# Feature-major products with act hi and lo as one 512-column operand in four banks

## The chip, the cores and the metric

The kernel runs on one core of a Trainium2 chip. The time is device microseconds of that core for one execution of the whole program; lower is better. Of the engines, PE does the matrix products (PEld are its weight loads), DVE and ACT the elementwise work, SP starts the transfers from device memory.

## The reference, cut to what matters

Two layers over 256 tokens of width 2048, all in float32. Layer A is a stick-breaking attention with 16 heads of 128, layer B a latent attention whose keys and values come from a compressed latent of 512.

```python
def mixer_a(h, w_in, w_out):
    q, k, v, g = jnp.split(h @ w_in, 4, axis=-1)
    o = stick_breaking_attention(heads(q), heads(k), heads(v)).reshape(b, s, SB_WIDTH)
    return (o * jax.nn.silu(g)) @ w_out
...
def mixer_b(h, kv, w_in, q_latent_norm, w_uq, w_out, cos, sin):
    cq, g = jnp.split(h @ w_in, [Q_LORA_RANK], axis=-1)
    q = (rms_norm(cq, q_latent_norm) @ w_uq).reshape(b, s, MLA_HEADS, QK_HEAD_DIM)
...
    o = mla_attention(q_nope, q_rope, k_nope, k_rope, v).reshape(b, s, MLA_WIDTH)
    return (o * jax.nn.silu(g)) @ w_out
...
for each layer:
    out = mixer(rms_norm(x, norm_pre))
    x = x + rms_norm(out, norm_post)
    x = x + (p @ w_ple_proj) * jax.nn.sigmoid(x @ w_ple_gate)
```

## The kernel before, in words

**Numbers in two parts.** PE multiplies in a reduced float32 (fp32r). Each operand is therefore held as hi, the rounded value, and lo, what is missing: `split` makes hi by an ACT copy and lo by a DVE subtraction (lines 81 to 87). A product is hi·hi + hi·lo + lo·hi: `mm3` (line 108) issues these three matmuls, lines 109 to 111, onto the same part of a PSUM bank.

**Units.** Weights come in units of 128 x 1024 floats (512 KB). `unit` (line 89) starts the transfer on SP into one of four `raw` buffers, then ACT makes `whi` and DVE `wlo`, four buffers each. Eight units make one group: 2048 rows of weights by 512 columns, which are four blocks of 128 columns (four heads). One unit holds two of the 16 row slices k.

**Two kinds of product.** `rows` (line 113) gives token-major results: activations are loaded as weights, 512 weight columns move, one bank per 128 tokens. `cols` (line 123) gives feature-major results: a 128 x 128 weight block is loaded and the 256 tokens move, so that two blocks share one bank of 512 floats. It runs over k outside and the four blocks inside, and all blocks of a group end with the last unit. `cols` makes the gates of both layers (`gate_group`, and the three loops from line 239), k and q of layer A (`group_a`, line 330) and the products with `w_uk` and `w_uq` (`group_b`, line 545, one unit for two blocks at four k). `rows` makes v, the outputs, the latents and the other gates.

**PSUM.** There are eight banks, four named `acc` and four `att`. A `cols` group takes two `acc` banks, so two groups fit; the third gate group of layer A takes two `att` banks (line 256). Behind a group, DVE multiplies each bank by a row of rms factors, 512 columns at a time (lines 221 and 337), or copies it (line 550); a gate then gets its silu on ACT (line 223).

**Activations.** `act_t` (line 161) holds the transposed activations, all of hi and then all of lo: [128, 2, 16, 256]. `latT` (line 488) does the same for the two latents.

**Order.** The program text gives each instruction its priority; the order on each engine's queue is set at build time by a scheduler that, whenever an engine comes free in its simulated time, takes the earliest instruction that is ready there. On the chip every queue is then served in that order. `weave` (line 136) lays three steps of each of the last group's four heads between the units of the next group: for layer A after units 1, 7, 13 and 19 and two and four units later.

Of the kernel before, what the change touches and what calls it, by code (L numbers as in the profile page):

```python
# [9 lines left out]
F32 = mybir.dt.float32  # L10
F32R = mybir.dt.float32r
BF16 = mybir.dt.bfloat16
AF = mybir.ActivationFunctionType
ALU = mybir.AluOpType
AX = mybir.AxisListType

P = 128
# [29 lines left out]
def hybrid_trunk(ctx: ExitStack, tc: tile.TileContext, a: dict):  # L47
# [11 lines left out]
    def acc():  # L59
        return psum.tile([P, SLAB], F32, tag="acc", name="acc", bufs=4)  # L60
# [59 lines left out]
            ts = slice(t * P, (t + 1) * P)  # L120
            mm3(accs[t], aT[0][:, k, ts], aT[1][:, k, ts], hi[:, c], lo[:, c], k == 0, k == ktot - 1)

    def cols(banks, aT, w, k0, nk, nblk, ktot):

        hi, lo = w
        for kk in range(nk):
            k = k0 + kk
            for i in range(nblk):
                c = slice((kk * nblk + i) * P, (kk * nblk + i + 1) * P)
                mm3(banks[i // 2][:, i % 2 * T:(i % 2 + 1) * T], hi[:, c], lo[:, c], aT[0][:, k, :], aT[1][:, k, :],  # L130
                    k == 0 and i % 2 == 0, k == ktot - 1 and i % 2 == 1, skip_group_check=True)

    def pair(ap):
        return ap.rearrange("p (k t) -> p k t", k=2)
# [24 lines left out]


    def act_t():
        b = big.tile([P, 2, NK, T], F32R, tag="actT", name="actT", bufs=2)
        return b[:, 0], b[:, 1]

    def transpose_pair(j):

# [42 lines left out]

    silus = []  # L210

    def gate_group(g, aT, sg, get, row):
        o = [acc(), acc()]
        for u in range(8):
            cols(o, aT, get(u), 2 * u, 2, GRP, NK)
        gate_out(g, o, sg, row)

    def gate_out(g, o, sg, row):
        for i in range(2):
            gt = tmp.tile([P, 2, T], F32, tag="t512", name="gt", bufs=2)  # L220
            nc.vector.tensor_tensor(gt, pair(o[i]), row, ALU.mult)
            h = g * GRP + 2 * i
            silus.append(nc.scalar.activation(sg[:, h:h + 2, :], gt, AF.Silu))

    def warm_up(n):

# [7 lines left out]
    hT = act_t()  # L234
    xs = big.tile([P, NK, T], F32, tag="tok", name="xs", bufs=3)
    sgA = big.tile([P, NH, T], F32, tag="sg", name="sgA", bufs=1)
    o0, o1 = [acc(), acc()], [acc(), acc()]
    warm_up(WARM)
    for u in range(8):
        nc.sync.dma_start(out=xs[:, 2 * u:2 * u + 2, :], in_=pair(a["xT"][u]))  # L240
        w = unit_ga(0, u, parts=2 if u == 0 else 1)
        for k in (2 * u, 2 * u + 1):
            split_gain(hT[0][:, k, :], hT[1][:, k, :], xs[:, k, :], pre[:, 0, k:k + 1])
        cols(o0, hT, w, 2 * u, 2, GRP, NK)

    ssq0 = ssq_tile("ssq0")
    c1 = const.tile([P, P + NK + 2 * NR + NT * 2 * ROPE], F32, name="c1")
    c2 = tmp.tile([P, 2 * P + CHUNK], F32, tag="e", name="c2", bufs=2)
    for u in range(8):
        cols(o1, hT, unit_ga(1, u), 2 * u, 2, GRP, NK)  # L250
        if u in (1, 4, 7):
            load_x(u // 3)
        if u == 6:
            after(nc.sync.dma_start(out=c1, in_=a["c1"]), loads[-1], "the weights go first")
    ident = c1[:, :P]
    o2 = [att(), att()]
    for u in range(8):
        cols(o2, hT, unit_ga(2, u), 2 * u, 2, GRP, NK)
        if u == 0:
            after(nc.sync.dma_start(out=c2, in_=a["c2"]), loads[-1], "the weights go first")  # L260
        if u == 2:
            load_x(3)
        if u == 4:
            rstd0 = rstd_of(ssq0, D, "rstd0")
            rrow0 = rstd_row(rstd0)
            gate_out(0, o0, sgA, rrow0)
            gate_out(1, o1, sgA, rrow0)
    gate_out(2, o2, sgA, rrow0)
    rrow0q = tmp.tile([P, 2, T], F32, tag="rrow", name="rrow0q", bufs=2)
    nc.vector.tensor_scalar(rrow0q, rrow0, SCALE_A, None, ALU.mult)  # L270

# [7 lines left out]
    trir = const.tile([P, P], F32R, name="trir")  # L279
    nc.vector.tensor_copy(trir, c2[:, :P])  # L280

    gate_group(3, hT, sgA, lambda u: unit_ga(3, u), rrow0)


    W3 = T + P
# [3 lines left out]
    after(exp_ln, silus[-1], "the table set of the attention comes after the gates'")  # L289

    def finish_head(h, o, sg, yT):
        y = tmp.tile([P, T], F32, tag="t256", name="y", bufs=2)
        nc.vector.tensor_tensor(y, o, sg[:, h, :], ALU.mult)
        split(yT[0][:, h, :], yT[1][:, h, :], y)

# [33 lines left out]

    def group_a(g, q, k, v):  # L330
        for dst, base, row in ((k, NG, rrow0), (q, 0, rrow0q)):
            o = [acc(), acc()]
            for u in range(8):
                cols(o, hT, unit(a["w_in_a"][(base + g) * 8 + u]), 2 * u, 2, GRP, NK)
                yield
            for i in range(2):
                nc.vector.tensor_tensor(dst[:, 2 * i:2 * i + 2, :], pair(o[i]), row, ALU.mult)
        o = [acc(), acc()]
        for u in range(8):
            rows(o, hT, unit(a["w_in_a"][(2 * NG + g) * 8 + u]), 2 * u, 2, SLAB, NK)  # L340
            yield
        for t in range(NT):
            nc.scalar.activation(v[:, t, :], o[t], AF.Copy, scale=rstd0[:, t:t + 1])
# [118 lines left out]
    def rotate(dst, src, t, n):  # L462

        hw = ROPE // 2
        cs = rope[:, t, 0:1, :].to_broadcast([P, n, ROPE])
        nc.vector.tensor_tensor(dst, src, cs, ALU.mult)
        u = tmp.tile([P, GRP, ROPE], F32, tag="t256", name="rot", bufs=2)[:, :n, :]
        for lo_, hi_ in ((0, hw), (hw, 0)):
            sn = rope[:, t, 1:2, lo_:lo_ + hw].to_broadcast([P, n, hw])
            nc.vector.tensor_tensor(u[:, :, lo_:lo_ + hw], src[:, :, hi_:hi_ + hw], sn, ALU.mult)  # L470
        nc.vector.tensor_tensor(dst, dst, u, ALU.add)

    krt = tmp.tile([P, NT, 2, ROPE], F32, tag="t256", name="krt", bufs=2)
    for t in range(NT):
        rotate(krt[:, t, 0:1, :], ckv[:, t:t + 1, RANK:], t, 1)
        nc.vector.tensor_copy(krt[:, t, 1, :], krt[:, t, 0, :])
# [6 lines left out]

    sgB = big.tile([P, NH, T], F32, tag="sg", name="sgB", bufs=1)
    for g in range(NG):
        gate_group(g, x2T, sgB, lambda u: unit_b(1 + g, u), rrow2)

    latT = big.tile([P, 2, 2, NR, T], F32R, tag="tok", name="latT", bufs=3)
    for i, src in ((0, ckv), (1, cq)):
        sl = ssq_tile(f"sl{i}", 1)  # L490
        for t in range(NT):
            sumsq(sl[:, t, :], src[:, t, :RANK])
        rl = rstd_of(sl, RANK, f"rl{i}")
        for t in range(NT):
            nc.vector.tensor_scalar(src[:, t, :RANK], src[:, t, :RANK], rl[:, t:t + 1], None, ALU.mult)
        for j in range(NR // 2):
            b = att()
            for kk in range(2):
                k = 2 * j + kk
                for t in range(NT):  # L500
                    nc.tensor.transpose(b[:, kk * T + t * P:kk * T + (t + 1) * P], src[:, t, k * P:(k + 1) * P], ident)
            for kk in range(2):
                k = 2 * j + kk
                split_gain(latT[:, i, 0, k, :], latT[:, i, 1, k, :], b[:, kk * T:(kk + 1) * T], qln[:, i, k:k + 1])
    ckvT, cqT = [(latT[:, i, 0], latT[:, i, 1]) for i in range(2)]


    yT = act_t()
# [36 lines left out]
    def group_b(g, q, qr, k, v):  # L545
        for dst, src, aT in ((k, a["w_uk"], ckvT), (q, a["w_uq"], cqT)):
            for i in range(GRP // 2):
                o = acc()
                cols([o], aT, unit(src[g * (GRP // 2) + i]), 0, NR, 2, NR)
                nc.vector.tensor_copy(dst[:, 2 * i:2 * i + 2, :], pair(o))  # L550
                yield
        w = unit(a["w_uqr"][g])
        o = [acc()[:, :T], acc()[:, :T]]
# [123 lines left out]
```

## Time and profile before

| | |
|---|---|
| median of 3 runs | 1056.81 us (1056.16 to 1056.97) |
| the profiled execution | 1058.96 us, its span 1057.2 us |
| granted clock of PE, mean | 0.998 |
| busy: PE, DVE, ACT | 1048.3, 608.9, 540.2 us |
| matmuls, and as many weight loads | 6715 |
| HBM | 178 GB/s over the span |

The profiled execution is 2.15 us longer than the median; 1.76 us of it lie outside the span. Matmuls overlap in the records, so PE's busy time says only that PE had something to do; what one costs is read from the distance between starts.

### The profile page before, as it was taken

To read this page: it belongs to the slowest core of one execution; us is meant where nothing else is said; L and a number is where in the kernel's file an instruction comes from. 1 tells how busy PE (TensorE), PEld (TensorE's weight loads), DVE (VectorE), ACT (ScalarE), POOL (GpSimd) and SP (SyncE) were. 2 spreads that over 40 slices of the span, in tenths; PEclk is the share of its full clock that TensorE was granted. 3 is DMA by queue.
4 is the path that set the end of the run, shared out by engine and by line. 5 is a ranking of instruction groups with operands and counts; after the bars stand their busy time and mean duration, and the time that the engine had idled before them with its cause. 6 is when DMAs were issued, how large, how long until landed. Compare 5 with 4: busy or idle time off the path is not lost.

```text
span 1057.2 us, 16656 instructions
## 1 busy us (share of the span) xinstructions
PE 1048.3 (99%) x6715; PEld 954.1 (90%) x6715; DVE 608.9 (58%) x832; ACT 540.2 (51%) x792; POOL 6.8 (1%) x10
## 2 busy tenths in 40 slices
PE   8999999999999999999999999999999999999998
PEld 7999999989989988888888899999999988788888
DVE  6455444554554545555766576555777765558554
ACT  6545334455445446545555565544555554446442
POOL 0000000000000000000000000000000000000000
PEclk9999999999999999999999999999999999999999
DMA  8855555555555554575665476656544344655662
GB/s 315 278 180 179 182 185 189 162 161 175 164 163 175 171 171 158 166 211 170 201 189 175 134 239 189 188 182 180 161 139 140 115 146 153 196 184 190 213 209 79
DMA packets 55821, 189.17 MB, mean 179 GB/s; under 512 B 6208, under 2 KB 6976, under 8 KB 55744
## 3 DMA queue, kind: packets, MB, share of 16 engines
q1 hardware_dynamic: 55600, 188.09, 56.8%
q8 instruction: 52, 0.85, 0.3%
q14 instruction: 25, 0.20, 0.1%
q10 hardware_dynamic: 144, 0.02, 0.0%
HBM read 185.99 MB, written 2.10 MB: 178 GB/s over the span
## 4 chain that ended last, share of the span: by engine, by line
PE 98%; DMA 1%; DVE 0%; ACT 0%; SPq 0%; issue 0%
PE acc L109 29%; PE acc L110 29%; PE acc L111 29%; PE att L300 1%; PE att L110 1%; PE att L111 1%; PE att L109 1%; PE att L171 1%; PE att L301 1%; PE att L518 1%; PE att L308 1%; DMA raw<-in_w_in_a_dram 1%; PE att L523 1%; PE att L539 0%; PE att L517 0%; PE att L324 0%
## 5 line engine op out<-in xcount | busy, mean ns | idle before, releaser
L83 DVE TENSOR_TENSOR wlo<-raw,whi 128x1024 fp32r<-128x1024 f32 (+1 forms) x295 | 358.5, 1217 | 306.0 <-ACT whi L82 305.3
L82 ACT ACTIVATE whi<-raw 128x1024 fp32r<-128x1024 f32 (+1 forms) x295 | 310.7, 1053 | 342.0 <-PE acc L111 177.8
L109 PE MATMUL acc<-whi,actT 128*128 128x512 f32 (+2 forms) x736 | 277.4, 378 | 0.8 <-DVE osb L390 0.8
L111 PE MATMUL acc<-whi,actT 128*128 128x512 f32 (+2 forms) x736 | 277.3, 378 | 0.0
L110 PE MATMUL acc<-wlo,actT 128*128 128x512 f32 (+2 forms) x736 | 277.1, 377 | 0.0
L109 PE MATMUL acc<-actT,whi 128*128 128x256 f32 x960 | 273.4, 285 | 1.5 <-ACT whi L82 1.5
L110 PE MATMUL acc<-actT,whi 128*128 128x256 f32 x960 | 272.5, 284 | 0.0
L111 PE MATMUL acc<-actT,wlo 128*128 128x256 f32 x960 | 271.5, 284 | 0.5 <-DVE wlo L83 0.5
L109 PEld LDWEIGHTS acc<-actT,whi 128*128 128x128 f32 x960 | 184.7, 192 | 2.5 <-ACT whi L82 2.4
L111 PEld LDWEIGHTS acc<-actT,wlo 128*128 128x128 f32 x960 | 184.3, 193 | 0.9 <-DVE wlo L83 0.9
L110 PEld LDWEIGHTS acc<-actT,whi 128*128 128x128 f32 x960 | 184.8, 192 | 0.1
L109 PEld LDWEIGHTS acc<-whi,actT 128*128 128x128 f32 x736 | 138.4, 188 | 25.1 <-DVE osb L390 1.2
L110 PEld LDWEIGHTS acc<-wlo,actT 128*128 128x128 f32 x736 | 138.5, 188 | 24.1
L111 PEld LDWEIGHTS acc<-whi,actT 128*128 128x128 f32 x736 | 138.2, 188 | 24.1
L87 DVE SCALAR_TENSOR_TENSOR wlo<-raw,pre,whi 128x512 fp32r<-128x512 f32 x80 | 56.8, 748 | 41.6 <-ACT whi L86 41.6
L86 ACT ACTIVATE whi<-raw,pre 128x512 fp32r<-128x512 f32 x80 | 53.5, 715 | 49.7 <-PE acc L110 28.6
L110 PE MATMUL acc<-latT,whi 128*128 128x256 f32 x128 | 36.4, 286 | 0.3 <-DVE latT L87 0.3
L111 PE MATMUL acc<-latT,wlo 128*128 128x256 f32 x128 | 36.4, 286 | 0.0
L109 PE MATMUL acc<-latT,whi 128*128 128x256 f32 x128 | 36.2, 287 | 0.2 <-ACT latT L86 0.2
L110 PEld LDWEIGHTS acc<-latT,whi 128*128 128x128 f32 x128 | 24.4, 191 | 0.5 <-DVE latT L87 0.5
L109 PEld LDWEIGHTS acc<-latT,whi 128*128 128x128 f32 x128 | 24.2, 191 | 0.4 <-ACT latT L86 0.4
L111 PEld LDWEIGHTS acc<-latT,wlo 128*128 128x128 f32 x128 | 24.4, 191 | 0.0
(236 smaller groups left out, 958.6 us busy)
## 6 DMA issues: line engine op xcount, KB each, us to landing
raw<-in_w_in_a_dram SPq DMA_DIRECT2D x127, 512.0 KB, 3.6
raw<-in_w_in_b_dram SPq DMA_DIRECT2D x40, 512.0 KB, 3.9
raw<-in_w_out_a_dram SPq DMA_DIRECT2D x32, 512.0 KB, 3.7
raw<-in_w_pg_a_dram SPq DMA_DIRECT2D x32, 512.0 KB, 3.6
raw<-in_w_out_b_dram SPq DMA_DIRECT2D x32, 512.0 KB, 3.6
raw<-in_w_pg_b_dram SPq DMA_DIRECT2D x24, 512.0 KB, 3.6
raw<-in_w_dkv_dram SPq DMA_DIRECT2D x16, 288.0 KB, 2.9
raw<-in_w_pp_dram SPq DMA_DIRECT2D x8, 512.0 KB, 3.6
```

The costliest lines, as they stand in the source:

```text
L82: nc.scalar.activation(hi, src, AF.Copy)
L83: nc.vector.tensor_tensor(lo, src, hi.bitcast(F32), ALU.subtract)
L86: nc.scalar.activation(hi, src, AF.Copy, scale=gain)
L87: nc.vector.scalar_tensor_tensor(lo, src, gain, hi.bitcast(F32), ALU.mult, ALU.subtract)
L109: nc.tensor.matmul(out, lhsT=sh, rhs=mh, start=start, stop=False, **kw)
L110: nc.tensor.matmul(out, lhsT=sh, rhs=ml, start=False, stop=False, **kw)
L111: nc.tensor.matmul(out, lhsT=sl, rhs=mh, start=False, stop=stop, **kw)
L171: nc.tensor.transpose(b[:, kk * T + t * P:kk * T + (t + 1) * P], x[:, t, k * P:(k + 1) * P], ident)
L300: nc.tensor.matmul(o, lhsT=v[:, 0, c], rhs=w[:, :T], start=True, stop=False)
L301: nc.tensor.matmul(o[:, P:], lhsT=v[:, 1, c], rhs=w[:, T:], start=False, stop=True)
L308: mm(z[:, :T], lhsT=k[:, hh, :P], rhs=q[:, hh, :], start=True, stop=False, skip_group_check=True)
L518: mm(s[:, P:], lhsT=q[:, hh, P:], rhs=k[:, hh, :], start=False, stop=False, skip_group_check=True)
```

## The change

The activations are stored by k, with hi and lo beside each other: [128, 16, 2, 256]. `cols` multiplies the hi part of a weight block with both at once, 512 columns into a whole bank, the left half hi·hi and the right half hi·lo; the lo part of the block is multiplied with act hi, 256 columns, onto the left half. One block now fills one bank, a group four. The new `halves` copies the right half out of the bank on ACT and adds the left half to it on DVE, into the destination; the row factor is then applied in place in SBUF. `cols` now runs over blocks outside and k inside. `cols_stream` gives it one unit at a time, but units 0 and 1 together, and 6 and 7 together: there a block's products over four k stand in a row before the next block's. Gate group 0 of layer A, which loads its activations with its weights, goes unit by unit. `halves` uses a third `t256` buffer, and gate group 2 of layer A uses `acc` banks.

```diff
-    def cols(banks, aT, w, k0, nk, nblk, ktot):
-        hi, lo = w
-        for kk in range(nk):
-            k = k0 + kk
-            for i in range(nblk):
-                c = slice((kk * nblk + i) * P, (kk * nblk + i + 1) * P)
-                mm3(banks[i // 2][:, i % 2 * T:(i % 2 + 1) * T], hi[:, c], lo[:, c], aT[0][:, k, :], aT[1][:, k, :],
-                    k == 0 and i % 2 == 0, k == ktot - 1 and i % 2 == 1, skip_group_check=True)
+    def cols(banks, aT, ws, k0, nk, ktot):
+        n = len(banks)
+        for i, o in enumerate(banks):
+            for m in range(len(ws) * nk):
+                hi, lo = ws[m // nk]
+                k = k0 + m
+                c = slice((m % nk * n + i) * P, (m % nk * n + i + 1) * P)
+                nc.tensor.matmul(o, lhsT=hi[:, c], rhs=aT[2][:, k].rearrange("p i t -> p (i t)"), start=k == 0,
+                                 stop=False, skip_group_check=True)
+                nc.tensor.matmul(o[:, :T], lhsT=lo[:, c], rhs=aT[0][:, k, :], start=False, stop=k == ktot - 1,
+                                 skip_group_check=True)
+    def cols_stream(banks, aT, get):
+        for us in ((0, 1), (2,), (3,), (4,), (5,), (6, 7)):
+            cols(banks, aT, [get(u) for u in us], 2 * us[0], 2, NK)
+            for _ in us:
+                yield
+    def halves(dst, banks):
+        for i, o in enumerate(banks):
+            b = tmp.tile([P, T], F32, tag="t256", name="half", bufs=3)
+            nc.scalar.copy(b, o[:, T:])
+            nc.vector.tensor_tensor(dst[:, i, :], o[:, :T], b, ALU.add)
...
     def act_t():
-        b = big.tile([P, 2, NK, T], F32R, tag="actT", name="actT", bufs=2)
-        return b[:, 0], b[:, 1]
+        b = big.tile([P, NK, 2, T], F32R, tag="actT", name="actT", bufs=2)
+        return b[:, :, 0, :], b[:, :, 1, :], b
...
     silus = []
-    def gate_group(g, aT, sg, get, row):
-        o = [acc(), acc()]
-        for u in range(8):
-            cols(o, aT, get(u), 2 * u, 2, GRP, NK)
-        gate_out(g, o, sg, row)
-    def gate_out(g, o, sg, row):
+    def banks4():
+        return [acc() for _ in range(GRP)]
+    def gate_group(g, aT, sg, get):
+        o = banks4()
+        for _ in cols_stream(o, aT, get):
+            pass
+        halves(sg[:, GRP * g:GRP * (g + 1), :], o)
+    def gate_out(g, sg, row):
...
-            gt = tmp.tile([P, 2, T], F32, tag="t512", name="gt", bufs=2)
-            nc.vector.tensor_tensor(gt, pair(o[i]), row, ALU.mult)
-            h = g * GRP + 2 * i
-            silus.append(nc.scalar.activation(sg[:, h:h + 2, :], gt, AF.Silu))
+            h = sg[:, GRP * g + 2 * i:GRP * g + 2 * i + 2, :]
+            nc.vector.tensor_tensor(h, h, row, ALU.mult)
+            silus.append(nc.scalar.activation(h, h, AF.Silu))
...
-    o0, o1 = [acc(), acc()], [acc(), acc()]
+    o = banks4()
...
     for u in range(8):
...
-        cols(o0, hT, w, 2 * u, 2, GRP, NK)
+        cols(o, hT, [w], 2 * u, 2, NK)
+    halves(sgA[:, :GRP, :], o)
...
-    for u in range(8):
-        cols(o1, hT, unit_ga(1, u), 2 * u, 2, GRP, NK)
+    o = banks4()
+    for u, _ in enumerate(cols_stream(o, hT, lambda u: unit_ga(1, u))):
         if u in (1, 4, 7):
...
         if u == 6:
...
-    o2 = [att(), att()]
-    for u in range(8):
-        cols(o2, hT, unit_ga(2, u), 2 * u, 2, GRP, NK)
+    halves(sgA[:, GRP:2 * GRP, :], o)
+    o = banks4()
+    for u, _ in enumerate(cols_stream(o, hT, lambda u: unit_ga(2, u))):
         if u == 0:
...
         if u == 2:
...
         if u == 4:
...
-            gate_out(0, o0, sgA, rrow0)
-            gate_out(1, o1, sgA, rrow0)
-    gate_out(2, o2, sgA, rrow0)
+            gate_out(0, sgA, rrow0)
+            gate_out(1, sgA, rrow0)
+    halves(sgA[:, 2 * GRP:3 * GRP, :], o)
+    gate_out(2, sgA, rrow0)
...
-    gate_group(3, hT, sgA, lambda u: unit_ga(3, u), rrow0)
+    gate_group(3, hT, sgA, lambda u: unit_ga(3, u))
+    gate_out(3, sgA, rrow0)
...
-        y = tmp.tile([P, T], F32, tag="t256", name="y", bufs=2)
+        y = tmp.tile([P, T], F32, tag="t256", name="y", bufs=3)
...
     def group_a(g, q, k, v):
...
-            o = [acc(), acc()]
-            for u in range(8):
-                cols(o, hT, unit(a["w_in_a"][(base + g) * 8 + u]), 2 * u, 2, GRP, NK)
-                yield
+            o = banks4()
+            yield from cols_stream(o, hT, lambda u: unit(a["w_in_a"][(base + g) * 8 + u]))
+            halves(dst, o)
...
-                nc.vector.tensor_tensor(dst[:, 2 * i:2 * i + 2, :], pair(o[i]), row, ALU.mult)
+                d = dst[:, 2 * i:2 * i + 2, :]
+                nc.vector.tensor_tensor(d, d, row, ALU.mult)
...
         for u in range(8):
...
-        u = tmp.tile([P, GRP, ROPE], F32, tag="t256", name="rot", bufs=2)[:, :n, :]
+        u = tmp.tile([P, GRP, ROPE], F32, tag="t256", name="rot", bufs=3)[:, :n, :]
...
-    krt = tmp.tile([P, NT, 2, ROPE], F32, tag="t256", name="krt", bufs=2)
+    krt = tmp.tile([P, NT, 2, ROPE], F32, tag="t256", name="krt", bufs=3)
...
-        gate_group(g, x2T, sgB, lambda u: unit_b(1 + g, u), rrow2)
-    latT = big.tile([P, 2, 2, NR, T], F32R, tag="tok", name="latT", bufs=3)
+        gate_group(g, x2T, sgB, lambda u: unit_b(1 + g, u))
+        gate_out(g, sgB, rrow2)
+    latT = big.tile([P, 2, NR, 2, T], F32R, tag="tok", name="latT", bufs=3)
...
-                split_gain(latT[:, i, 0, k, :], latT[:, i, 1, k, :], b[:, kk * T:(kk + 1) * T], qln[:, i, k:k + 1])
-    ckvT, cqT = [(latT[:, i, 0], latT[:, i, 1]) for i in range(2)]
+                split_gain(latT[:, i, k, 0, :], latT[:, i, k, 1, :], b[:, kk * T:(kk + 1) * T], qln[:, i, k:k + 1])
+    ckvT, cqT = [(latT[:, i, :, 0, :], latT[:, i, :, 1, :], latT[:, i]) for i in range(2)]
...
     def group_b(g, q, qr, k, v):
...
-                o = acc()
-                cols([o], aT, unit(src[g * (GRP // 2) + i]), 0, NR, 2, NR)
-                nc.vector.tensor_copy(dst[:, 2 * i:2 * i + 2, :], pair(o))
+                o = [acc(), acc()]
+                cols(o, aT, [unit(src[g * (GRP // 2) + i])], 0, NR, NR)
+                halves(dst[:, 2 * i:2 * i + 2, :], o)
```

## Rows read from the trace of the kernel before

**Rows 1.** The page, busy us of each engine, share of the span, instructions.

```profile
PE 1048.3 (99%) x6715; PEld 954.1 (90%) x6715; DVE 608.9 (58%) x832; ACT 540.2 (51%) x792; POOL 6.8 (1%) x10
```

**Rows 2.** The page, chain that ended last, share of the span by line.

```profile
PE acc L109 29%; PE acc L110 29%; PE acc L111 29%; PE att L300 1%; PE att L110 1%; PE att L111 1%; PE att L109 1%; PE att L171 1%; PE att L301 1%; PE att L518 1%; PE att L308 1%; DMA raw<-in_w_in_a_dram 1%; PE att L523 1%; PE att L539 0%; PE att L517 0%; PE att L324 0%
```

**Rows 3.** Waits of PE: who waited for whom, us in total, times, longest.

```profile
PE acc L109 <- ACT whi L82: 1.5, 2, 1.3
PE att L229 <- DVE zeros L149: 1.2, 1, 1.2
PE acc L109 <- DVE osb L390: 0.8, 1, 0.8
PE acc L111 <- DVE wlo L83: 0.5, 1, 0.5
```

**Rows 4.** Windows: length, busy us (instructions) of PE, PEld, DVE, ACT, POOL; clock, DMA.

```profile
25.00:120.00 95.00, 95.00 (x794) 95.00 (x794) 47.43 (x50) 44.95 (x58) 0.69 (x1) 1.00 0.65 210
120.00:400.00 280.00, 280.00 (x1950) 262.97 (x1949) 142.76 (x154) 133.66 (x171) 0.00 (x0) 1.00 0.56 173
740.00:860.00 120.00, 119.56 (x860) 111.03 (x859) 86.45 (x188) 68.26 (x137) 0.00 (x0) 1.00 0.47 142
```

**Rows 5.** Groups by line and form: count, busy us, mean ns; idle before.

```profile
L109 PE MATMUL acc<-actT,whi 128*128 128x256 f32 x960 | 273.4, 285 | 1.5 <-ACT whi L82 1.5
...
L109 PE MATMUL acc<-latT,whi 128*128 128x256 f32 x128 | 36.2, 287 | 0.2 <-ACT latT L86 0.2
L109 PE MATMUL att<-actT,whi 128*128 128x256 f32 x64 | 18.2, 284 | 0.0
```

**Rows 6.** Window, PE alone: us, busy, matmuls, granted clock, DMA share, GB/s.

```profile
655.00:735.00 80.00, 80.00 (x669) 1.00 0.60 185
```

**Rows 7.** Timeline of PE where kinds meet: start, recorded length, instruction.

```profile
148.33 0.28 PE L111 MATMUL acc<-actT,wlo 128*128 128x256 f32 x1
148.45 0.40 PE L109 MATMUL acc<-whi,actT 128*128 128x512 f32 x1
148.68 0.40 PE L110 MATMUL acc<-wlo,actT 128*128 128x512 f32 x1
148.92 0.39 PE L111 MATMUL acc<-whi,actT 128*128 128x512 f32 x1
...
170.01 0.39 PE L111 MATMUL acc<-whi,actT 128*128 128x512 f32 x1
170.24 0.28 PE L109 MATMUL acc<-actT,whi 128*128 128x256 f32 x1
170.35 0.28 PE L110 MATMUL acc<-actT,whi 128*128 128x256 f32 x1
```

**Rows 8.** Groups by line and form, DVE and ACT.

```profile
L83 DVE TENSOR_TENSOR wlo<-raw,whi 128x1024 fp32r<-128x1024 f32 x291 | 355.7, 1224 | 303.4 <-ACT whi L82 302.8
L82 ACT ACTIVATE whi<-raw 128x1024 fp32r<-128x1024 f32 x291 | 308.1, 1059 | 338.2 <-PE acc L111 174.5 <-PE acc L110 135.3 <-issue 12.0
...
L550 DVE COPY arena<-acc 128x512 f32<-128x512 f32 x16 | 11.0, 688 | 8.3 <-PE acc L111 8.1
...
L531 ACT ACTIVATE pr<-att,st 128x256 f32<-128x256 f32 x16 | 7.5, 471 | 0.0
...
L293 DVE TENSOR_TENSOR y<-att,sgA 128x256 f32<-128x256 f32 x16 | 6.8, 424 | 15.3 <-PE att L301 15.3
```

**Rows 9.** Timeline of ACT in group 1: first and last of one attention step.

```profile
193.51 0.47 ACT L313 ACTIVATE e<-att 128x384 f32<-128x384 f32 x1
...
195.72 0.53 ACT L82 ACTIVATE sph<-sp 128x384 fp32r<-128x384 f32 x1 [0.62 <-DVE sp L317]
```

**Rows 10.** Timeline of PE at the first product with `w_uk`.

```profile
742.66 0.39 PE L110 MATMUL acc<-latT,whi 128*128 128x256 f32 x1 [0.28 <-DVE latT L87]
```

**Rows 11.** Timeline of DVE where k of group 0 ends.

```profile
124.89 1.41 DVE L337 TENSOR_TENSOR qkvA<-acc,rrow 128x512 f32<-128x512 f32 x2
126.58 1.23 DVE L83 TENSOR_TENSOR wlo<-raw,whi 128x1024 fp32r<-128x1024 f32 x1 [0.28 <-ACT whi L82]
```

## The prediction

> **What bounds the kernel now.** I read the busy times of the page first [rows 1]: PE is busy 99% of the span, DVE 58%, ACT 51%. The chain that ended last says the same more strictly [rows 2]: 87% of the span lies on lines 109 to 111, the three products of `mm3`, and the rest of that row is nearly all PE too. PE hardly ever waits: the four largest kinds of its waits come to 4.0 us, most of it at the start [rows 3]. In three stretches that the change touches (gates of A, heads of A, first part of the heads of B), PE is busy all the time or all but half a microsecond, while DVE stands at 50 to 72% [rows 4]. So the time is the sum of what PE's instructions take, and only a change in that sum, or a new wait of PE, can move the end.
>
> The mean duration of a matmul (285 ns for 256 columns [rows 5]) is not its price, since the records overlap. The price is the distance from start to start. From 655 to 735 us PE does nothing but feature-major products, 669 in 80.00 us [rows 6]: 119.6 ns each, and I use 120 ns. The token-major products with 512 moving columns start 0.23 us apart [rows 7]; a 256 with 0.11 to 0.12 beside them. I use 227 ns: 120 and the 107 ns that 256 more columns take at the granted clock (1.00, the 2.4 GHz level [rows 6]). So each of these instructions costs about 13 ns beside its columns, however many it has, with a weight load for each in both cases.
>
> **The change, part by part.**
>
> *Products.* Before, one weight block at one k takes three instructions of 256 columns: 3 x 120 = 360 ns. After, it takes one of 512 and one of 256: 227 + 120 = 347 ns. The columns stay the same; one instruction and its weight load are gone. Saved: 13 ns. How many: 960 into acc from actT, 128 from latT and 64 into att [rows 5], 1152 in all (gates 512, q and k of layer A 512, uk and uq 128). 1152 x 13 ns = **15.0 us**. The mixed order stands in the trace only where a group of one kind follows the other: a 256 and then a 512 at 148.33, a 512 and then a 256 at 170.01 [rows 7]. They start 0.12 and 0.23 us apart, so neither neighbour costs the other anything. The ends: with the dearest spacing of these rows (0.24 for a 512 and 0.12 for a 256) 360 ns and nothing is saved; with the cheapest (0.23 and 0.11) 340 ns and 23 us. I take 347 because the 669 products and the same differences on both sides of a transition stand behind it.
>
> *Copies and adds (`halves`).* Each block now needs a 256-column ACT copy out of its bank and a 256-column DVE add: 96 of each. Nearest rows: 471 ns for an ACT pass over 256 out of a bank, 424 ns for a DVE product of that size [rows 8]; I take 0.47 and 0.42 us. ACT gains 96 x 0.47 = 45 us, so 585 us of some 1042, 56%. DVE gains 96 x 0.42 = 40 us less the 16 copies of 0.69 us [rows 8] that go, so some 638 us, 61%. The products with the rms row stay, from SBUF instead of a bank. The tightest stretch, 740 to 860 us, holds 32 of the adds and loses the 16 copies: 86.5 + 13.4 - 11.0 = 89 us of 117, 76%. No queue becomes the bound; the work is hidden under PE, and without that cover the 85 us would count.
>
> *Banks.* A gate, k or q group held two of four accumulator banks, and the next group took the other two. Now it holds all four, and the next group's block i waits for bank i. There are 16 such turnovers: four behind the gates of A, four from k to q, four from q to v, four behind the gates of B. What hides them is the block order at both ends: a pair of units is 16 x 0.347 = 5.55 us, the banks fall due 1.39 us apart, and each is wanted 4.16 us after its last product. Copy and add take 0.89 us; behind one weight split on each queue (1.06 and 1.22 us [rows 8]) they take 3.17 us, which fits. Where an attention step stands ahead on ACT (Abs to the split of sp, 193.51 to 196.25 us, 2.74 us [rows 9]), it is 5.9 us, 1.7 too late. That can meet the three turnovers from k to q in groups 1 to 3, where the first step of a head is due in unit 7. Lower end 0, upper end 5 us; I take 0.5, since ACT has gaps between these steps. After group 0 of the gates, whose last unit is not paired, the banks fall due 0.69 us apart and the first has 2.1 us: it fits with one split half done.
>
> *Units.* A pair wants its second unit 2.2 us earlier and gives both weight buffers back at its end. Four buffers: at a turnover two are held by units 6 and 7 and two by the next 0 and 1, which were split in the buffers of 4 and 5, long free. Units 2 and 3 are split only when the pair ends; they are ready about 2.3 and 3.5 us later, and unit 2 is wanted 5.55 us later. With the last add and two row products on DVE ahead (0.42 + 1.38) it is 4.1 us. I cost it at nothing; it is late by 0.65 us if everything, an attention step's 2 us of DVE too, stands before both splits.
>
> *Order.* The pairs move head steps one unit later, and c2's load on SP behind one more weight load; x's third and c1's loads likewise at most one unit. Nobody needs them within 2.8 us, so nothing. The third `t256` buffer costs no time. At the start PE waits for arriving weights (1.5 and 0.5 us [rows 3]); the first unit is taken block by block, which may cost or give up to 0.8 us; I take 0.
>
> *Into uk.* At 742.66 a product already waited 0.28 us for the latent's split [rows 10]. The two last gate units now release their weight buffers together, so one more split on each queue (up to 2.3 us) can stand ahead of the latent's. Ends 0 and 2.3; I take 0.5, the wait that this row shows, near twice over.
>
> **Sum**, against the profiled execution's own 1058.96 us: -15.0 + 0.5 + 0.5 = 1044.96. The runs' median, 1056.81, is 2.15 us below the profiled one, so **1042.8 us**, 1.3% faster. A measurement of this kernel tells some 0.2% (2.1 us) from no change.
>
> **Rivals.**
>
> 1. *The turnover takes the place of the saving: slower.* If the four copies stand on ACT behind a weight split that is itself released only by the pair's end, the stagger is lost: block 0 of the next group waits for a split, a copy and an add, 1.06 + 0.47 + 0.42 = 1.95 us. Times 16 that is 31 us: 1042.8 - 0.5 + 31 = 1073. It decides from 15/16 = 0.94 us per turnover on. For it: ACT's queue is served in order, and no group has a spare bank. Against it: the evacuation of k at 124.89 started before the next split on DVE at 126.58 [rows 11], and the copies come first in the program. Chance 0.06. The Trainium skill (Perfetto Trace Analysis, Optimizing Tensor Performance) speaks for this rival: independent groups should rotate through different banks so that one's evacuation overlaps the next one's products. By that rule the change gives up an overlap that the kernel before has.
>
> 2. *Units or banks come late, but little: still faster.* At each turnover both splits are 0.65 us late: 10 us, so 1042.8 + 10 = 1053. For it: DVE's share rises everywhere. Against it: slack of 1.4 us or more without attention work. Chance 0.09.
>
> 3. *The change does not save what it says.* If a 512 that alternates with a 256 costs 240 ns, the pair costs the old 360 ns, and with 1 us of new waits the time is 1058. Against it: the two transitions [rows 7], where a 512 before a 256 takes 0.23. Chance 0.05. The Trainium skill (TensorE: Matmul & The Clock Gate, Back-to-back issue gap) gives an isolated gap of N/2.4 + 2.5 ns; by it an instruction saved would be worth 2.5 ns, an estimate of 2.9 us in all and a time near 1055. The trace does not agree: 13 ns beside the columns in 669 products [rows 6].
>
> **How the numbers follow.** Forecast 0.80, rivals 0.06, 0.09 and 0.05. The forecast's own range goes from 1039.5 (no new wait, and the waits at the start, 3.2 us [rows 3], shrink by 2) to 1047 (5 us at the turnovers). To hold 8 in 10 I go up to 1050, half of the second rival. Faster by over 0.2%: 0.80 and most of rival 2, 0.88. Within 0.2%: the third and the rest of the second, 0.06. Slower: the first, 0.06.
>
> **What would show it.** Right: feature-major stretches show a 512 and a 256 starting 347 ns apart in sum; PE's instructions fall by 1152; its waits stay near 5 us. Wrong: PE waits on ACT copies or DVE adds at the first product of a group (rival 1), on wlo at units 1 to 3 (rival 2), or a pair takes 360 ns (rival 3).

## The result and the profile after

The changed kernel takes **1045.94 us** (median of 4 runs, 1045.87 to 1046.15), the kernel before 1056.53 us beside it (4 runs, 1056.16 to 1056.97). The ratio is 0.99, 95% interval 0.9883 to 0.9917. That is 10.6 us less where the prediction said 14.0, so the direction and the range hold and the size is 3 us short. The profiled execution took 1045.87 us, with a span of 1044.1.

The page's busy times of the kernel after (engine, busy us, share, instructions), beside [rows 1]:

```profile
PE 1035.8 (99%) x5563; PEld 890.4 (85%) x5563; DVE 630.6 (60%) x912; ACT 567.4 (54%) x888; POOL 6.9 (1%) x10
```

PE has 1152 instructions fewer, as many as there are merged pairs. DVE gained 80 and ACT 96, and PE is still the one engine with hardly any idle time. The chain that ended last, by line, beside [rows 2]:

```profile
PE acc L133 24%; PE acc L109 17%; PE acc L111 17%; PE acc L110 17%; PE acc L135 12%; PE att L325 1%; DMA raw<-in_w_in_a_dram 1%; PE att L191 1%; DMA x<-in_x_dram 1%; PE att L544 1%; PE att L333 1%; PE att L326 1%; PE att L549 1%; PE att L565 0%; PE att L109 0%; PE att L111 0%
```

L133 is the merged product, L135 the one that is left. Together they hold 36% of the span; `mm3` (L109 to L111) keeps the token-major half, 51%. No copy (L150) stands in the chain and only one add (L151), 0.44 us at 29.46, behind gate group 0. PE's waits (who for whom, us in total, times, longest), beside [rows 3]:

```profile
PE att L251 <- DVE zeros L169: 1.2, 1, 1.2
PE acc L133 <- ACT whi L82: 1.1, 2, 0.7
PE acc L133 <- DVE actT L87: 0.5, 1, 0.5
PE att L325 <- ACT pT__7336 L567: 0.5, 1, 0.5
PE att L325 <- ACT pT__6987 L567: 0.5, 1, 0.5
```

The first three lie at the start, as before. The two on `pT` are new, 1.0 us together. The 0.8 us on `osb` in [rows 3] is gone. Three windows (length, busy us and instructions of PE, PEld, DVE, ACT, POOL, granted clock, DMA share, GB/s), beside [rows 4]; the last one lies 5 to 10 us earlier because the stage does:

```profile
25.00:120.00 95.00, 94.86 (x546) 82.69 (x545) 53.96 (x70) 49.84 (x78) 0.69 (x1) 1.00 0.65 221
120.00:400.00 280.00, 280.00 (x1504) 241.53 (x1504) 156.51 (x188) 146.30 (x209) 0.00 (x0) 1.00 0.54 174
735.00:850.00 115.00, 114.05 (x696) 100.06 (x696) 82.05 (x195) 72.04 (x155) 0.00 (x0) 1.00 0.45 146
```

PE is idle for 0.14 us in the first and 0.95 us in the last, with 31% and 23% fewer instructions in the first two. DVE goes from 50% to 57% and from 51% to 56% of its windows, ACT from 47 or 48% to 52%. In the last window, the tightest for DVE, it stands at 71%, where 76% was forecast. The groups by line and form (count, busy us, mean ns, idle before), beside [rows 5, 8]:

```profile
L133 PE MATMUL acc<-actT,whi 128*128 128x512 f32 x1024 | 356.1, 398 | 1.7 <-ACT whi L82 1.1 <-DVE actT L87 0.5
L135 PE MATMUL acc<-actT,wlo 128*128 128x256 f32 x1024 | 273.2, 281 | 0.1
...
L150 ACT COPY half<-acc 128x256 f32<-128x256 f32 x96 | 34.6, 367 | 35.3 <-PE acc L135 33.4 <-DVE actT L83 1.6
L151 DVE TENSOR_TENSOR qkvA<-acc,half 128x256 f32<-128x256 f32 x32 | 13.5, 421 | 5.7 <-ACT half L150 5.7
```

A copy takes 367 ns where 470 was estimated, an add 421 as estimated. The timeline of PE (start, recorded length, instruction), first in a stretch of gate group 2, then in one near the end of gate group 3, beside [rows 7]:

```profile
59.92 0.39 PE L133 MATMUL acc<-actT,whi 128*128 128x512 f32 x1
60.15 0.28 PE L135 MATMUL acc<-actT,wlo 128*128 128x256 f32 x1
60.27 0.39 PE L133 MATMUL acc<-actT,whi 128*128 128x512 f32 x1
60.50 0.28 PE L135 MATMUL acc<-actT,wlo 128*128 128x256 f32 x1
60.62 0.39 PE L133 MATMUL acc<-actT,whi 128*128 128x512 f32 x1
60.85 0.28 PE L135 MATMUL acc<-actT,wlo 128*128 128x256 f32 x1
60.96 0.39 PE L133 MATMUL acc<-actT,whi 128*128 128x512 f32 x1
...
94.56 0.40 PE L133 MATMUL acc<-actT,whi 128*128 128x512 f32 x1
94.79 0.28 PE L135 MATMUL acc<-actT,wlo 128*128 128x256 f32 x1
94.91 0.40 PE L133 MATMUL acc<-actT,whi 128*128 128x512 f32 x1
95.14 0.28 PE L135 MATMUL acc<-actT,wlo 128*128 128x256 f32 x1
95.26 0.40 PE L133 MATMUL acc<-actT,whi 128*128 128x512 f32 x1
95.50 0.28 PE L135 MATMUL acc<-actT,wlo 128*128 128x256 f32 x1
95.62 0.40 PE L133 MATMUL acc<-actT,whi 128*128 128x512 f32 x1
```

Here is the lesson of this case. Three pairs take 1.04 us in the first stretch, 347 ns each, which is the forecast. In the second they take 1.06 us, 353 ns each. PE waits in neither, and the clock is 1.00 in both. The starts in ns show two patterns: the first pace goes 350, 343, 350, 343 (or 347, 346), the second 361, 349, 350, 361, 349, 350, and a pace holds for some 3 to 20 us. Of the 924 pairs that another merged product follows at once, 37 hold a pause or a wait (430 ns and more); the mean of the other 887 is 349.5 ns, in a second profile of this kernel 349.8; I use 349.7. A 512 before a 256 takes 233 of them.

The pace is no accident of one execution. From 58 us on, 809 of 810 pairs have the same length within 2 ns in the second profile. And within a stretch in which 512 and 256 alternate strictly, it does not change: in none of the 41 such stretches of seven pairs or more (696 pairs) of the first profile, and in one of 41 of the second. The scheduler has not laid all pairs strictly in turn; the changes lie where two products of one size follow each other, where another kind of product comes between, or at a pause.

### The profile page after: what moved, and what is told of

Its sections match the earlier page's. It is cut to its first block, busy times and chain, and to the rows that moved or that the text cites. A ratio compares the mean times of both kernels' runs of the same rounds, so it can differ in the third digit from the quotient of the medians.

```text
span 1044.1 us, 14568 instructions
## 1 busy us (share of the span) xinstructions
PE 1035.8 (99%) x5563; PEld 890.4 (85%) x5563; DVE 630.6 (60%) x912; ACT 567.4 (54%) x888; POOL 6.9 (1%) x10
## 4 chain that ended last, share of the span: by engine, by line
PE 96%; DMA 2%; DVE 1%; ACT 0%; issue 0%; SPq 0%; DVEq 0%
PE acc L133 24%; PE acc L109 17%; PE acc L111 17%; PE acc L110 17%; PE acc L135 12%; PE att L325 1%; DMA raw<-in_w_in_a_dram 1%; PE att L191 1%; DMA x<-in_x_dram 1%; PE att L544 1%; PE att L333 1%; PE att L326 1%; PE att L549 1%; PE att L565 0%; PE att L109 0%; PE att L111 0%
## 5 line engine op out<-in xcount | busy, mean ns | idle before, releaser
L133 PE MATMUL acc<-actT,whi 128*128 128x512 f32 x1024 | 356.1, 398 | 1.7 <-ACT whi L82 1.1
L111 PE MATMUL acc<-whi,actT 128*128 128x512 f32 (+2 forms) x736 | 277.6, 379 | 0.0
L109 PE MATMUL acc<-whi,actT 128*128 128x512 f32 (+2 forms) x736 | 277.1, 378 | 0.0
L135 PE MATMUL acc<-actT,wlo 128*128 128x256 f32 x1024 | 273.2, 281 | 0.1
L133 PEld LDWEIGHTS acc<-actT,whi 128*128 128x128 f32 x1024 | 189.2, 188 | 40.9 <-ACT whi L82 2.6
L135 PEld LDWEIGHTS acc<-actT,wlo 128*128 128x128 f32 x1024 | 192.6, 189 | 6.1 <-DVE wlo L83 0.7
L109 PEld LDWEIGHTS acc<-whi,actT 128*128 128x128 f32 x736 | 138.4, 188 | 24.0
L111 PEld LDWEIGHTS acc<-whi,actT 128*128 128x128 f32 x736 | 138.2, 188 | 23.9
L150 ACT COPY half<-acc 128x256 f32<-128x256 f32 x96 | 34.6, 367 | 35.3 <-PE acc L135 33.4
L133 PE MATMUL acc<-latT,whi 128*128 128x512 f32 x128 | 46.2, 401 | 0.0
L135 PE MATMUL acc<-latT,wlo 128*128 128x256 f32 x128 | 36.0, 282 | 0.0
L133 PEld LDWEIGHTS acc<-latT,whi 128*128 128x128 f32 x128 | 24.0, 188 | 5.7 <-DVE arena L151 0.4
L135 PEld LDWEIGHTS acc<-latT,wlo 128*128 128x128 f32 x128 | 24.2, 189 | 0.1
L82 ACT ACTIVATE actT<-y 128x256 fp32r<-128x256 f32 x32 | 13.3, 418 | 19.6 <-DVE y L318 19.3
L109 PE MATMUL acc<-whi,latT 128*128 128x256 f32 (+1 forms) x64 | 21.8, 340 | 0.0
L557 ACT ACTIVATE pr<-att,st 128x128 f32<-128x128 f32 (+1 forms) x32 | 13.3, 424 | 15.6 <-DVE st L555 15.6
```

The lines of the kernel that those rows point to most:

```text
L82: nc.scalar.activation(hi, src, AF.Copy)
L109: nc.tensor.matmul(out, lhsT=sh, rhs=mh, start=start, stop=False, **kw)
L111: nc.tensor.matmul(out, lhsT=sl, rhs=mh, start=False, stop=stop, **kw)
L133: nc.tensor.matmul(o, lhsT=hi[:, c], rhs=aT[2][:, k].rearrange("p i t -> p (i t)"), start=k == 0, stop=False, skip_group_check=True)
L135: nc.tensor.matmul(o[:, :T], lhsT=lo[:, c], rhs=aT[0][:, k, :], start=False, stop=k == ktot - 1, skip_group_check=True)
L150: nc.scalar.copy(b, o[:, T:])
```

## Experiments

**What of the 10.6 us is the change?** The profiled execution of before was 2.15 us above its median, so the kernel before ran once more.

> The kernel before, profiled once more. Theory A: its first profiled execution (1058.96 us, span 1057.2) was long by chance, by some 2.4 us against the median of 1056.5, and 1.8 us always lie outside the span: the span comes out near 1054.8 us, and one or two waits of PE of the first profile are shorter, at the start (1.54 us between two products at 8.30) or at 904.9 (1.21 us). Theory B: a profile always costs this kernel 2.4 us: the span is 1057 again with the same waits, and the change saved 13 us in a like-for-like comparison.

It took 1056.38 us, with a span of 1054.6. Windows of PE at the start (length, busy us and instructions, granted clock, DMA share, GB/s), the first profile of before:

```profile
8.00:12.00 4.00, 2.22 (x14) 0.91 1.04 414
12.00:15.00 3.00, 3.00 (x17) 0.55 1.04 400
```

and the same kernel again:

```profile
8.00:12.00 4.00, 3.43 (x26) 1.00 1.03 412
12.00:15.00 3.00, 3.00 (x27) 1.00 1.06 405
```

In the first, PE was idle for 1.8 of 4 us, and from 12 to 15 us the granted clock was then 0.55, close to the lower of its two levels (1.2 GHz): 17 products where the second ran 27. The extra 2.15 us were a disturbed start of that one execution and no part of the kernel. Like for like the spans are 1054.6 and 1044.1: **10.5 us**, which the medians confirm.

**What is the merge alone worth?** Everything of the change stays (four banks, copies, adds, order), but the 512 is two 256s again:

```diff
-nc.tensor.matmul(o, lhsT=hi[:, c], rhs=aT[2][:, k]..., start=k == 0, ...)
+nc.tensor.matmul(o[:, :T], lhsT=hi[:, c], rhs=aT[0][:, k, :], start=k == 0, ...)
+nc.tensor.matmul(o[:, T:], lhsT=hi[:, c], rhs=aT[1][:, k, :], start=False, ...)
```

> The changed kernel with the 512-column product taken apart again into two of 256 (act hi into the left half, act lo into the right), all else as changed. My theory (the merge itself saves 360 minus 349.7 ns, which is the mean start-to-start time of the pairs in the changed trace, and all else is free): 1045.9 + 1152 x 10.3 ns = 1057.8 us, about the kernel before plus 1. Rival (the merge saves the forecast 13 ns or more and banks, copies and pairs give 3 us back): 1061 us or more.

1059.16 us (9 runs), ratio 1.0024 [1.0014, 1.0033]. That lies between the two theories. The merge is worth 1059.16 - 1045.94 = 13.2 us, and the rest of the change by itself costs 2.5 us (1056.66 before, beside it). Its products start 120 ns apart throughout. Its largest new waits of PE:

```profile
PE acc L133 <- DVE arena L153: 1.9, 3, 0.7
PE acc L133 <- DVE sgB L153: 0.5, 1, 0.5
```

These waits on adds into uk, uq and the gates of B come to 2.4 us; the kernel after has none of them. By the distances between starts, the feature-major products of this kernel take 421.7 us, 12.0 more than in the kernel after (409.7), and all other products 1.3 more; against the kernel before (second profile) they take 1.8 and 1.0 more. So the saving comes from the merged instruction, as forecast, and the evacuation alone would have been a loss. The two kernels differ in one thing more: the scheduler lays out the queues anew for each. Here the transposes of the latent stand at 737 to 739 us, just ahead of `w_uk`, as in the kernel before, and PE waits there; in the kernel after they stand at 661 to 707 us. So a part of the 13.2 us is the new order, and that part was not measured by itself.

**Is the block order what hides the evacuation?** First without the pairs, then also with k outside and the blocks inside, so that all four banks of a group end within its last four pairs:

```diff
-for us in ((0, 1), (2,), (3,), (4,), (5,), (6, 7)):
+for us in ((0,), (1,), (2,), (3,), (4,), (5,), (6,), (7,)):
...
-for i, o in enumerate(banks):
-    for m in range(len(ws) * nk):
+for m in range(len(ws) * nk):
+    for i, o in enumerate(banks):
```

> The changed kernel with every unit by itself, blocks outside and k inside, so that a bank is wanted 2.08 us after its last product and not 4.16. My theory (an evacuation takes 0.8 us, in the way stands at most one split): 0 to 0.4 us at each of 16 turnovers, 1046 to 1052 us, likeliest 1048. Rival (the turnovers are what eats the missing 3 us, and half the cover makes it much worse): over 1 us at each, 1061 us or more.

> The changed kernel in the loop order of before: every unit by itself, k outside and the four blocks inside, so that all four banks of a group fall due within its last 1.04 us and all four are wanted within the next group's first 1.04 us. If the block order is what hides the evacuation: copy and add of four banks one behind the other (0.37 + 4 x 0.42 = 2.05 us) are exposed by about 1 us at each of 16 turnovers, more where a split of 1.06 or 1.22 us stands ahead: 1058 to 1075 us, likeliest 1062. Rival (PE finds other work or the banks come free in time anyway): within 2 us of 1046.

Without pairs (the first line alone): 1046.41 us, ratio 0.9898 [0.9882, 0.9915], at most 0.8 us dearer than the kernel after (1045.94 in one set, 1045.59 in another). With k outside as well: 1049.21 us, ratio 0.9928 [0.9913, 0.9943], only 3.3 to 3.6 us dearer, where 12 to 29 were expected. The timeline of PE shows two turnovers of this second kernel, from gate group 0 to 1 and after the gates:

```profile
28.85 0.27 PE L135 MATMUL acc<-actT,wlo 128*128 128x256 f32 x1
31.99 0.50 PE L133 MATMUL acc<-actT,whi 128*128 128x512 f32 x1 [2.87 <-DVE sgA L151]
...
101.24 0.28 PE L135 MATMUL acc<-actT,wlo 128*128 128x256 f32 x1
101.38 0.50 PE L133 MATMUL acc<-actT,whi 128*128 128x512 f32 x1
```

and that of ACT beside them:

```profile
27.92 0.63 ACT L200 ACTIVATE junk<-x 128x512 bf16<-128x512 f32 x1 [3.42 <-DMA x<-in_x_dram]
...
29.30 1.04 ACT L82 ACTIVATE whi<-raw 128x1024 fp32r<-128x1024 f32 x1
30.25 0.90 ACT L150 COPY half<-acc 128x256 f32<-128x256 f32 x3
...
100.49 1.09 ACT L150 COPY half<-acc 128x256 f32<-128x256 f32 x3 [0.83 <-PE acc L135]
```

One turnover costs 2.9 us, of the 4.0 us by which this execution (1049.90 us, the longest of its four) exceeds the profiled one of the kernel after: ACT had waited 3.42 us for x, and the squares of x and a weight split stood ahead of the copies. The other costs about 0.1 us, although the banks end only 0.35 us apart: there the copies are first on ACT and pick up each bank as it ends. The turnovers between the other groups cost at most 0.2 us each by the starts. So the wait that was feared is real, but in this kernel it came only where a queue was late for another reason. That holds it to one place, and block order is a cover for that place.

**How much ACT can the copies take?** Each copy twice:

```diff
 nc.scalar.copy(b, o[:, T:])
+nc.scalar.copy(b, o[:, T:])
```

> The changed kernel with each of the 96 ACT copies out of a bank done twice, some 35 us more on ACT and 0.37 us later release of each bank. If copies and adds lie wholly beside PE's work, as forecast: within 1 us of the changed kernel, 1045 to 1047. Rival (they are in PE's way at the turnovers): 16 x 0.37 us = 6 us or more, 1052.

> The changed kernel once more, timed beside the others of this set: 1045.9 us within 0.5.

The doubled kernel took 1048.61 us (1047.26 to 1051.76), the kernel after beside it 1045.59 (1045.44 to 1046.12): 3.0 us for 35 us more of ACT, between the two theories. The profiled execution is the shortest of the four, 1.8 us above its counterpart. PE's waits on the banks in it:

```profile
PE acc L133 <- DVE sgA L152: 1.6, 1, 1.6
PE acc L133 <- DVE arena L152: 1.0, 2, 0.8
```

The copies lie beside PE at their single size, but for 0.4 us behind gate group 0; twice the size begins to show, at three turnovers, most at that same one (1.6 us).

**Why 349.7 and not 347?** The first theory: each seam between a 512 and a 256 costs something, so long runs of one size would give 3 us back. All 512s of a unit go first, then all its 256s; per block where units are paired and at the end of a group (first kernel), with no pairs (second), with all units in pairs (third):

```diff
-for m in range(len(ws) * nk):
-    matmul(o, hi ...); matmul(o[:, :T], lo ...)
+for part in range(2):
+    for i, j in run:
+        if part == 0: matmul(o, hi ...)
+        else: matmul(o[:, :T], lo ...)
```

> The changed kernel with the two kinds of product grouped: all 512-column products of a unit and then all its 256-column ones (per block, four and four, in the paired units and in the last unit of a row sum). Theory A (a 512 that alternates with a 256 costs some 3 ns per pair more than each among its own kind, 349.7 against 226.7 + 120.0 ns): the pairs come down to about 347 ns, 1152 x 3 ns less a few at the seams, 1043 us. Theory B (the 3 ns belong to the 512-column product from actT itself, whatever stands beside it): 1045.9 us within 0.5, and the 512s still start 230 ns apart among themselves.

> As the run with grouped products, and every unit by itself (no pairs). The pairs were worth 0.5 us or nothing with alternating products. Here a unit's last eight products of 120 ns end the four banks 0.24 us apart outside the last unit only; the last unit still goes block by block, so a bank is wanted some 2 us after its end: 1043 to 1044.5 us if theory A holds, 1046 to 1047 if theory B holds.

> The grouped kernel with longer runs: units in pairs throughout, sixteen 512-column products and then sixteen of 256 in the first three pairs of a group, four and four in the last. In the grouped run each seam from 256 to 512 columns cost some 20 ns (the next five 512s start 233, 236, 229, 232 and 231 ns apart and then 227, the first 256 takes 113), which is as much as alternating costs over eight pairs. Theory of the seams: 3 + 4 seams per group in place of 8 + 4, 5 x 20 ns x 16 groups = 1.6 us less than the grouped run's 1045.2: 1043.6 us. Rival (the extra is not tied to seams, or the pairs of units come late): 1045 us or more.

1045.17 us (1044.97 to 1045.39), 1045.57 (1045.27 to 1046.15) and 1045.55 (1044.91 to 1045.95). The best of them is 0.4 us below the kernel after in its set, none gives 3 us. The timeline of PE in the first (xcount instructions that follow one another in a row):

```profile
17.47 2.00 PE L137 MATMUL acc<-actT,whi 128*128 128x512 f32 x8
19.31 1.11 PE L140 MATMUL acc<-actT,wlo 128*128 128x256 f32 x8
20.26 1.09 PE L137 MATMUL acc<-actT,whi 128*128 128x512 f32 x4
```

Eight 512s take 1.84 us and eight 256s 0.95, together 2.79, so 349 ns for each pair although there is one seam in eight of before. The single distances in such a run of 512s are 233, 236, 229, 232, 231, 227, 226 and 227 ns: after the seam the 512s start wide apart and settle at 227 only with the sixth. One change from 256 to 512 and back costs some 20 ns beside the steady 227 and 120 in long runs, and 3 ns when the sizes alternate: an eighth of the changes in this unit, at over six times the price. The third kernel shows the same price in its runs of sixteen:

```profile
85.98 3.82 PE L137 MATMUL acc<-actT,whi 128*128 128x512 f32 x16
89.64 2.08 PE L140 MATMUL acc<-actT,wlo 128*128 128x256 f32 x16
91.55 0.63 PE L137 MATMUL acc<-actT,whi 128*128 128x512 f32 x2
```

Sixteen pairs take 5.57 us, 348 ns each (347.7 over all undisturbed runs of sixteen). But the last quarter of each group, in runs of four, stands at 350.0 ns, and the 1.6 us that were expected do not show in the time. So a change of size has its price, and long runs pay it less often, but no order that was tried brings all pairs to 347.

Next, what the 512 reads. One kernel moves 512 columns of weights instead of activations, one loads activations instead of weights, and one keeps the kernel before's layout, so that the 512 columns are two separate runs of 256 (the first two compute another product):

```diff
-matmul(o, lhsT=hi[:, c], rhs=aT[2][:, k]...)
+matmul(o, lhsT=hi[:, c], rhs=hi[:, m % 2 * SLAB:(m % 2 + 1) * SLAB])
...
+matmul(o, lhsT=aT[0][:, k, i % 2 * P:(i % 2 + 1) * P], rhs=aT[2][:, k]...)
...
+matmul(o, lhsT=hi[:, c], rhs=aT[2][:, :, k, :])   # act_t: [P, 2, NK, T]
```

> The changed kernel, but the 512-column product moves 512 columns of the unit's own whi instead of the activations (weight block still loaded; the result is another product). In the changed kernel this product takes 233.3 ns before a 256 and 231.7 ns among its own kind, in the token-major products 226.7. Theory M (it is what moves, the activations): the product falls to about 227 to 228 ns, the pair to some 345, the time to about 1041 us. Theory L (it is what is loaded, whi): still 233, 1046 us.

> The changed kernel, but the 512-column product loads 128 columns of act hi as weights instead of the block of whi, which no product reads (the 256-column one still loads wlo; the result is another product). Theory L: the product falls to about 227 to 228 ns, some 1041 us. Theory M: still 233, 1046 us.

> The changed kernel with the activations stored as before, all of hi and then all of lo, so that the 512 moving columns are two runs of 256 that lie 16 KB apart. If the extra 5 ns of this product came from the place of its columns, the time moves: a second run may cost a few ns more for each of 1152, 1047 to 1051 us. If only the number of columns counts: 1045.6 within 0.5, and the new layout was not needed.

The first took 1045.21 us (one run). Its timeline of PE:

```profile
92.10 0.40 PE L133 MATMUL acc<-whi 128*128 128x512 f32 x1
92.33 0.28 PE L135 MATMUL acc<-actT,wlo 128*128 128x256 f32 x1
92.45 0.40 PE L133 MATMUL acc<-whi 128*128 128x512 f32 x1
92.69 0.28 PE L135 MATMUL acc<-actT,wlo 128*128 128x256 f32 x1
92.81 0.40 PE L133 MATMUL acc<-whi 128*128 128x512 f32 x1
```

Two pairs in 0.71 us, and a 512 before a 256 takes 233 ns on average, as with activations. The second took 1050.06 us (one run); its products come to wait on other tiles, 6.1 us in the four largest kinds beside the warm-up's, where all of these waits in the kernel after are 2.7. Its 512s before 256s take 233.5. The third took 1045.39 us, ratio 0.9886 [0.987, 0.9903], against 1045.94 and 1045.59 for the layout of the change. In the first and the third, PE's products stand in the order of the kernel after, and so do the paces: 790 and 800 of 810 pairs from 58 us on have the same length within 2 ns. In the second the order is another, and only 402 of 744 pairs agree. So it is neither what is moved, nor what is loaded, nor where it lies, and the new layout of `act_t` and `latT` is not needed for the gain.

## Why the prediction was right, and where its size was off

The account, from the distances between starts of PE's products in the second profile of before and the one of after: feature-major products 419.9 to 409.7 us (-10.2), token-major products 546.1 to 545.0 (-1.0), all others 78.7 to 79.6 (+0.9), the warm-up -0.2. Sum -10.5, the difference of the spans. The forecast was 14.0.

*Products: the right mechanism, and the one term that was mis-sized.* 1152 blocks were right, 360 ns before was right (119.9 ns a product measured; the products of the kernel with three of 256 too), 227 + 120 = 347 was not: 349.7 is measured, so 1152 x 10.3 = 11.9 us instead of 15.0. This is 3.1 us, as much as the forecast missed in all; what else it missed, both ways, nearly cancels, which is luck. "Neither neighbour costs the other anything" rested on one transition each way [rows 7], read to 10 ns; the excess is 3 ns a pair, which rows of that resolution cannot show. The two bounds, 340 and 360 ns, held it. The other 1.7 us of the feature-major difference (-11.9 to -10.2) are small places: the turnover at 29.5 (0.4), the start (0.6), pauses of some 80 ns of which there are a few more, and the rounding of 119.9 to 120; the waits at `w_uk` that went count 0.6 the other way.

*Copies and adds: right.* 96 of each, 367 and 421 ns, beside PE. ACT came to 567.4 us (585 said), DVE to 630.6 (638); where DVE is tightest, 71% (76% said). That cover has an end: doubled copies cost 3.0 us.

*Banks: right in sum (0.5 said, 0.4 found), and wrong about what carries it.* No turnover of the kernel after waits more than 0.4 us. The one that waits is behind gate group 0, of which the prediction said that it fits; the turnovers from k to q, for which it put 0.5 in the sum, show no wait. Near 98 us ACT does what rival 1 feared:

```profile
96.88 0.37 ACT L150 COPY half<-acc 128x256 f32<-128x256 f32 x1 [1.05 <-PE acc L135]
97.15 0.64 ACT L245 ACTIVATE sgA<-sgA 128x512 f32<-128x512 f32 x1
97.68 2.00 ACT L82 ACTIVATE whi<-raw 128x1024 fp32r<-128x1024 f32 x2
99.58 0.36 ACT L150 COPY half<-acc 128x256 f32<-128x256 f32 x1
```

The last copy stands behind a Silu and two weight splits, and PE doesn't wait, since that bank is wanted again 4.16 us after its last product and its add ends on DVE at 101.46, before that. But the runs without pairs show that most turnovers would do with far less: the cover is worth 0.8 us at most for the pairs and some 3 us for the block order, and 2.9 us were seen at one place.

*Units and order: right at nothing.* No wait on a split outside the start. *Into uk: 0.5 said, and it went the other way.* The wait of [rows 10] went instead of growing: the scheduler now lays the latent's transposes at 661 to 707 us, inside the gates, where before they stood at 740 us, just ahead of `w_uk`. The prediction had not reckoned with a new order there.

*Not foreseen, and equal:* the 0.8 us on `osb` [rows 3] is gone, and two waits of 0.5 us on ACT's copy of `pT` came, at 784 and 815 us, in the stretch of the heads of B where ACT holds the new copies. That these are the cause of the new waits was not tried.

*The baseline: right.* Taking 2.15 us off, because the profiled execution stood above the median, is borne out by the second profile: that time was in its start. The lower end of the range adds up to 1039.8, not 1039.5; nothing hangs on it.

*Rival 1* fell: its 0.94 us per turnover was reached at none of the kernel after. In the experiments it was reached behind gate group 0 with k outside (2.9 us) and with doubled copies (1.6), and just so behind the gates of B in the run that loads activations (0.96). The Trainium skill (Perfetto Trace Analysis, Optimizing Tensor Performance) asks for different banks for independent groups; here one group fills all four and pays 0.4 us, with banks that come due one by one. *Rival 2* fell: no late unit. *Rival 3* (a pair at 360 ns) fell, but it pointed at the right place: the price of mixing sizes. The Trainium skill (TensorE: Matmul & The Clock Gate, Back-to-back issue gap) would, by its isolated gap, make the saved instruction worth 2.5 ns, an estimate; the trace does not agree: measured are 10.3 ns from the starts, and 13.2 us / 1152 = 11.5 with the waits that went with it.

## What to carry to other kernels

Where PE is the bound and each product has about 13 ns beside its columns, fewer and wider products pay, even for an additional copy and add on engines that stand at 50 to 60%; price the work that this adds on its own (here 2.5 us without the merge). Price a new order of instructions from many starts of that same order, or give its term a range of some nanoseconds each: 3 ns x 1152 is as much as the whole miss. Before building an elaborate cover for a bank, look at which engine queue is late and where: one place asked for it, the others hardly did. And read from the trace whether the scheduler kept the order: a variant that changes one line of text can change the queues too.

## What was not expected of the hardware

Products of 512 and 256 columns, each steady by itself (227 and 120 ns), average 349.7 ns for a pair when mixed, in paces of about 347 and 353 ns, with the clock at 1.00 and no wait. The pace goes with the order of the products: it holds through a strict alternation (41 of 41 stretches of seven pairs or more in one profile, 40 of 41 in the other), and at the same place of the program it is nearly always the same in executions of kernels whose PE instructions stand in the same order. After a run of 256s, 512s take five products to come down from 233 to 227 ns.

Why one order runs at 347 and another at 353 is open: what is moved, what is loaded and where it lies were changed above without effect on the price of the 512 (233 ns), and in the trace both paces occur with ACT and DVE busy, with both idle, and at a DMA share of 0.93 to 0.94 (48 to 52 us at the first pace, 90 to 92.5 us at the second). An order that would keep all pairs at the first pace was not sought.
